# Moving the sums of a later stage from the stretches of two heads to those of two convolution groups

## The chip, the cores and the metric

The kernel runs on one core of a Trainium2 chip. The metric is device time in microseconds, the median of several executions of the whole program. One further execution was profiled; the trace and the profile page come from it. The engines are called as in the profile: PE (matrix products; PEld is its weight load), DVE, ACT, POOL, and SP, which only issues DMAs here.

## The reference

One layer of a hybrid decoder, on a sequence of 2048 rows of width 1024 with 16 learned rows in front. What is computed, cut to what matters:

```
hn   = rms_norm(h, norm1_g)
proj = einsum('bld,de->ble', hn, w_in)              # 1024 x 4096
cx, cb, cc, cg, q, k, v, rg = split(proj, 8)        # 512 columns each
conv_out = short_conv(cx, cb, cc, conv_w) * silu(cg)
qf, kf   = rotary(q) * 128**-0.5, rotary(k)
ret      = head_group_norm(retention_chunkwise(qf, kf, v), ret_norm_g)
mixed    = concat([conv_out, ret * silu(rg)])       # 1024 wide
h        = h + einsum('ble,ed->bld', mixed, w_out)
out      = rms_norm(h, final_g)[:, 16:]
```

Everything is float32. There are four retention heads of width 128, and the convolution half is worked in four groups of 128 channels.

## The kernel before

**Stages.** The sequence is worked in two rounds of 1024 rows, and then comes an output stage of eight pairs of 128-row tiles for `w_out`. A round has eight units: four heads (units 0 to 3, function `head`) and four convolution groups (units 4 to 7, function `conv_group`; unit 4 of the first round is `group_plain`). The order is (4, 0, 1, 2, 3, 5, 6, 7) in the first round and (0, ..., 7) in the second. A unit is two products of 256 columns of `w_in` with the 1024 rows, called quads. The profile has a quad's matmuls at line 215.

**Products.** Each float32 operand is split into a high part (ACT, line 102) and a low part (DVE, line 114 or 106), and three matmuls stand for one. A quad also saves one product in eight by a scheme of block sums (function `quad`, seven products of 12 matmuls): it needs sums and differences of the four blocks of each operand. On the side of the weights they are made for every quad, by POOL (function `stationary`, lines 136 to 139). On the other side they are made once for each 1024 rows: by `block_sums` (lines 167 to 182), which for each of four slices takes four blocks of 128x512 and makes four DVE operations of 128x512, and one scaling on ACT if a gain is to be applied.

**The sums of a later stage.** For the second round, and for the output stage, these sums are made ahead. The generator `prepare` (lines 184 to 192) makes one of four steps each time it is advanced: four loads of 256 KB, `block_sums`, and four stores to a DRAM buffer (line 191). In the first round it runs over the second half of the sequence (`sums_x`, with gain), in the second round over `w_out` (`sums_w`, no gain). `prepared` (lines 194 to 202) reads the buffers back at the start of the stage that uses them. For half of `sums_w` the second round's last unit has early copies into SBUF (tile `held`, line 892).

**Advancing it.** `later` is that generator. It is advanced in the loop over the units (lines 881 to 883), twice after each head but unit 0; it has four steps, so the calls after units 1 and 2 use them up and the calls after unit 3 do nothing. A head ends, as written, with the loads for the next unit and with its retention part, which runs on the engines beside the next unit's products. What is written down after a head, too, stands ahead of the next unit's instructions, and runs in that unit's stretch. Another generator, `steps` (line 867), makes the row factors of the second round in the first round's convolution groups: eight loads and eight squares on ACT (line 324) a group, at units 5 and 6.

**Order on the engines.** Every engine and SP work their instructions in a fixed order, made when the program is built: a planner simulates the program, and takes on each engine, among what it holds to be ready, what was written down first. So an instruction can run ahead of what was written before it if that isn't ready. All DMAs are issued by SP.

**Buffers.** The loads, the products of heads (`kv`, `qg`), and the tiles of the convolution (`u`, `c`) and of the row factors (`n`) share 16 buffers of one tag (`GEN`, function `gen`). Weights have 8 raw buffers (`RAW`), and three for each split part (`RING`).

Of the kernel before, what the change touches and what calls it, by code (L numbers as in the profile page):

```python
# [20 lines left out]
NG = 4  # L21
# [50 lines left out]
def hybrid_trunk(ctx: ExitStack, tc: tile.TileContext, t, out: bass.AP, chunk_decay):  # L72
# [23 lines left out]
    def brief(name="b"):  # L96
        return sb.tile([P, HB + 128], F32, name=name, tag="b", bufs=BRIEF)[:, :HB]
# [50 lines left out]
    def parts(m, i, kt, src, factor=None):  # L148
        hi, lo = operand(i, kt)
        split(hi, lo, src, factor)  # L150
        m[i].append((hi, lo))

    def moving(load, scale=None, after={}):


        m = [[] for _ in range(8)]
        blocks = []
        for j in range(2):
            for half in range(2):
                for kt in range(KH):  # L160
                    k = half * KH + kt
                    blocks.append(load(k, j))
                    parts(m, BLOCK[half][j], kt, blocks[-1], scale(k) if scale else None)
                    after.get((j, k), lambda: None)()
        return m, blocks

    def block_sums(b11, b12, b22, b21, t1, t3, f, g, eng=nc.vector):

        def less(out, a, factor, b):
            if factor is None:
                sub(nc.vector, out, a, b)
            else:
                nc.vector.scalar_tensor_tensor(out=out, in0=a, scalar=factor, in1=b, op0=ALU.mult, op1=ALU.subtract)

        if f is not None:
            nc.scalar.mul(b11, b11, f)
        less(t1, b12, f, b11)
        less(b22, b22, g, t1)  # L180
        less(b21, b21, g, b22)
        sub(eng, t3, b22, b11)
# [60 lines left out]
    def plain_part(n, load, slot):  # L243
        a = sb.tile([P, HB], F32, name="ra", tag="ra", bufs=RAW)
        load(a)
        hi, lo = operand(slot, n)
        split(hi, lo, a)
        return a, (hi, lo)

    def plain_parts(loads, slot=PLAIN_W):  # L250
        w = {n: plain_part(n, loads[n], slot)[1] for n in (0, 2, 1, 3)}
        return [w[n] for n in range(4)]
# [91 lines left out]
    def row_tile(name, pair):  # L344
        return sb.tile([P, BLK], F32, name=name, tag=f"rr{pair}", bufs=2)

    def row_factors(r, f):

        f.extend([row_tile("rr", r), row_tile("rr2", r), []])
        for j in range(2):  # L350
            ss = small.tile([P, 2, CH], F32, name="ss", tag="ss")
            for c in range(CH):
                row_squares(ss, r, j, c)
                yield
            f[2].append(spread_factors(ss, *(a[:, j * HB : (j + 1) * HB] for a in f[:2])))
        yield

    def gain_of(k):
        return gain[:, k : k + 1]

    def load_x(r):
        def load(k, j):
            a = gen("x")[:, :HB]
            nc.sync.dma_start(a, t["xT"][r, j, k])
            return a

        return load
# [25 lines left out]
    def meta_products(blocks, early=False):  # L393

        bank = ps_misc()
        four = [bank[i * 32 : i * 32 + NMETA, :P] for i in range(4)]
        with tc.high_priority(offset=HIGH) if early else nullcontext():
            for kt in range(KH):
                for i in (3, 2, 1, 0):
                    nc.tensor.matmul(  # L400
                        four[i], meta_s[:, i % 2 * KH + kt, :], blocks[i][:, kt * P : (kt + 1) * P],
                        start=kt == 0, stop=kt == KH - 1,
                    )
        scratch = sb.tile([P, HB], F32, name="mk", tag="tc", bufs=COPIES).rearrange("p (a c) -> p a c", a=CH)
        for i in range(4):
            nc.scalar.copy(out=scratch[:NMETA, i], in_=four[i])
        return scratch
# [30 lines left out]
    def w_loads(n):  # L438
        return [lambda a, i=i: nc.sync.dma_start(a, t["w_in"][n, i]) for i in range(4)]
# [375 lines left out]
    for r in range(NR):  # L815
        f = factors[r]
        rot_t = sb.tile([P, 2, BLK], F32, name="rot_t", tag="rot_t", bufs=1)
        p0 = NMETA + r * BLK

        def load_tables():  # L820
            nc.sync.dma_start(rot_t, t["rot"][:, :, p0 : p0 + BLK])

        if r == 0:
            w = [None] * 4
            loads = w_loads(2 * NG)

            def begin(half):
                for n in (half, 2 + half):
                    w[n] = plain_part(n, loads[n], FIRST_W)

            m, b = moving(
                load_x(r), gain_of, {(0, 0): lambda: begin(0), (0, KH - 1): lambda: begin(1), (0, KT - 1): normalise_meta}
            )
            first = [[p for a, p in w]]
            blocks = None, meta_products([a for a, p in w])
            first.append(plain_parts(w_loads(2 * NG + 1)))
            load_tables()
            nc.sync.dma_start(cols, t["cols"])
            t3 = [a[:, i * HB : (i + 1) * HB] for a in (row_tile("t3", 1) for _ in range(2)) for i in range(2)]
            t1 = [brief("t1") if n < BRIEF else sb.tile([P, HB], F32, name="t1", tag="tc", bufs=COPIES) for n in range(KH)]  # L840
            for kt in range(KH):
                b11, b21, b12, b22 = (b[n * KH + kt] for n in range(4))
                block_sums(b11, b12, b22, b21, t1[kt], t3[kt], gain_of(kt), gain_of(KH + kt), nc.gpsimd)
                parts(m, 2, kt, b22)
                parts(m, 6, kt, b21)
            for _ in row_factors(0, f):
                pass
            nc.sync.dma_start(causal, t["causal"])
            nc.sync.dma_start(conv_w, t["conv_w"])
            nc.sync.dma_start(ret_g, t["ret_norm_g"])  # L850

            def late_parts():
                for i, held in ((3, t1), (4, t3)):
                    for kt in range(KH):
                        parts(m, i, kt, held[kt])

            between = ()
            later = prepare(load_x(1), sums_x, gain_of)
        else:
            m, b = moving(load_x(r), gain_of)  # L860
            first = [plain_parts(w_loads(0))]
            load_tables()
            prepared(m, sums_x, (1, 3))
            between = (lambda: prepared(m, sums_x, (0, 2)),)
            blocks = None, None
            later = prepare(load_w_out, sums_w)
        steps = row_factors(r + 1, factors[r + 1]) if r < NR - 1 else iter(())
        units = UNITS[r]
        turning = None
        special = (first, between)  # L870
        for n, unit in enumerate(units):
            following = units[n + 1] if n + 1 < len(units) else None
            rest = lambda: ahead(r, following, early=n == 0)
            if r + n == 0:
                blocks, completion = group_plain(unit - NG, m, f, blocks[1], first, late_parts, rest)
                special = (), completion
            elif unit < NG:
                if turning is None:
                    turning = [row_tile(name, 1 - r) for name in ("apart", "across")]
                blocks = head(unit, r, m, rot_t, f, turning, blocks, rest, *(special if unit == 0 else ()))  # L880
                if unit > 0:
                    next(later, None)
                    next(later, None)
            else:
                if r == NR - 1 and following is None:
                    idle = sb.tile([P, 2, BLK], F32, name="held", tag="rot_t", bufs=1)
                    areas = [idle[:, 0], idle[:, 1], row_tile("held", 0), row_tile("held", 0)]
                    for i, a in enumerate(areas):
                        for j in range(2):
                            n, kt = 2 * (i // 2), i % 2 * 2 + j  # L890
                            held[n, kt] = a[:, j * HB : (j + 1) * HB]
                            nc.sync.dma_start(held[n, kt], sums_w[n, kt])
                blocks = conv_group(unit - NG, r, m, f, blocks, rest)
                for _ in range(4 - r):
                    next(steps, None)

    m, b = moving(load_w_out)
    final_g = row_tile("final_g", 1)
# [41 lines left out]
```

## Time and profile before

| | us |
|---|---|
| median of 3 runs (lowest to highest) | 887.29 (886.79 to 888.18) |
| the profiled execution's own time | 886.64 |
| its span, from the first to the last instruction | 884.9 |
| PE busy | 872.3 |
| DVE busy | 718.4 |
| POOL busy | 400.4 |

The granted clock of TensorE was 0.999 on average. The span is what the trace shows; the profiled execution's time has 1.7 us more around it. PE's matmuls are pipelined: one of line 215 has a duration of about 390 ns in the trace and the next starts 227 ns after it, so PE can show as busy while a matmul starts up to 0.16 us late.

Rows of a table by stretches are read like this: the stretch in us from the start of the span, its length, then for PE, PEld, DVE, ACT and POOL the busy time with the number of instructions in brackets, the granted clock, the share of the DMA engines, and GB/s. Rows of groups have line, engine, operation, tile written, tiles read, shapes and count, then busy time and mean ns of one, then the idle time before them and what ended it. Rows of the timeline begin with start and duration in us.

### The profile page before, as it was taken

The numbers are of one execution on the slowest core, as the hardware profiler recorded it, in microseconds if no ns is written. First come the engines' busy times: TensorE is split into PE (matmuls) and PEld (weight loads), VectorE is DVE, ScalarE is ACT, GpSimd is POOL, SyncE is SP. The second block draws the span as 40 slices with busy tenths as digits, with TensorE's granted clock in tenths as the row PEclk, the third lists the DMA queues.
The fourth block names the chain that finished last, engine by engine and source line by source line (L and its number), as shares of the span: only waits on it lengthen the run. The fifth ranks groups of instructions, "written<-read, shape, count | busy, mean of one in ns | idle before, by whom it ended". The sixth has DMA issues, their size and how long they took to land.

```text
span 884.9 us, 12802 instructions
## 1 busy us (share of the span) xinstructions
PE 872.3 (99%) x4343; PEld 717.7 (81%) x4343; DVE 718.4 (81%) x1176; ACT 441.1 (50%) x848; POOL 400.4 (45%) x291
## 2 busy tenths in 40 slices
PE   8999999999999999999999999999999999999996
PEld 5778788878888878888888888888888887788885
DVE  6888888989877866999899999877768699767763
ACT  8664426354545463836352534444334475555553
POOL 0554232323235554452223333354546445887773
PEclk9999999999999999999999999999999999999999
DMA  9721216455334343834236363325222493545531
GB/s 338 234 65 50 73 49 180 142 152 170 90 101 145 107 144 95 288 113 135 58 85 215 88 223 96 119 71 155 60 72 60 145 366 108 175 159 175 171 129 74
DMA packets 93137, 121.12 MB, mean 137 GB/s; under 512 B 24528, under 2 KB 41232, under 8 KB 93072
## 3 DMA queue, kind: packets, MB, share of 16 engines
q1 hardware_dynamic: 93072, 120.31, 43.0%
q8 instruction: 34, 0.56, 0.3%
q14 instruction: 31, 0.25, 0.1%
HBM read 90.92 MB, written 25.17 MB: 131 GB/s over the span
## 4 chain that ended last, share of the span: by engine, by line
PE 56%; DVE 6%; DMA 2%; issue 2%; ACT 1%; POOL 1%; SPq 0%; POOLq 0%; DVEq 0%; ACTq 0%
PE pj L215 50%; DVE ml L114 2%; PE pj L265 2%; DVE wl L114 1%; PE ms L682 1%; PE ms L669 1%; DVE ml L106 1%; PE ms L693 1%; PE ms L692 1%; DMA t<-sums_w 1%; DMA n<-in_x 1%; POOL yo L111 0%; DMA yo<-in_x 0%; DMA ra<-in_w_in 0%; DVE pm L709 0%
## 5 line engine op out<-in xcount | busy, mean ns | idle before, releaser
L215 PE MATMUL pj<-mh,wl 128*128 128x512 f32 x1008 | 398.7, 396 | 1.9 <-ACT tc L222 1.0
L215 PE MATMUL pj<-ml,wh 128*128 128x512 f32 x1008 | 393.2, 390 | 0.0
L215 PE MATMUL pj<-mh,wh 128*128 128x512 f32 x1008 | 392.7, 390 | 0.0
L102 ACT CAST wh<-ra 128x512 fp32r<-128x512 f32 x216 | 133.7, 620 | 260.9 <-PE pj L215 201.3
L215 PEld LDWEIGHTS pj<-mh,wl 128*128 128x128 f32 x1008 | 189.3, 188 | 44.7 <-ACT tc L222 2.8
L114 DVE TENSOR_TENSOR wl<-ra,wh 128x512 fp32r<-128x512 f32 x216 | 193.4, 898 | 39.3 <-ACT wh L102 38.9
L215 PEld LDWEIGHTS pj<-mh,wh 128*128 128x128 f32 x1008 | 189.2, 188 | 39.8
L215 PEld LDWEIGHTS pj<-ml,wh 128*128 128x128 f32 x1008 | 189.4, 188 | 37.9 <-issue 0.5
L114 POOL TENSOR_TENSOR ra<-ra 128x512 f32<-128x512 f32 x72 | 113.1, 1571 | 93.9 <-PE ms L400 40.9
L111 POOL TENSOR_TENSOR sa<-ra 128x512 f32<-128x512 f32 x36 | 55.2, 1533 | 100.0 <-DVE wl L114 46.7
L114 POOL TENSOR_TENSOR ra<-sa,ra 128x512 f32<-128x512 f32 x36 | 52.5, 1459 | 92.5 <-DVE wl L114 78.2
L222 ACT COPY tc<-pj 128x512 f32<-128x512 f32 x108 | 62.8, 581 | 0.0
L265 PE MATMUL pj<-ml,mh 128*128 128x512 f32 x128 | 50.2, 392 | 0.1
L265 PE MATMUL pj<-mh,mh 128*128 128x512 f32 x128 | 49.9, 393 | 0.0
L265 PE MATMUL pj<-mh,ml 128*128 128x512 f32 x128 | 48.8, 398 | 0.5 <-DVE ml L114 0.4
L525 POOL TENSOR_TENSOR c<-c,rr 128x512 f32<-128x512 f32 x14 | 27.8, 1984 | 26.8 <-DVE c L525 18.0
L705 POOL TENSOR_TENSOR rp<-rs,neg_half 128x4 f32<-128x4 f32 x16 | 19.4, 1215 | 43.4 <-DVE rs L111 43.4
L756 DVE TENSOR_TENSOR yo<-pj,yo 128x512 f32<-128x512 f32 x32 | 21.9, 687 | 17.9 <-PE pj L215 8.0
L102 ACT CAST wh<-sa 128x512 fp32r<-128x512 f32 x36 | 22.4, 621 | 27.5 <-PE pj L215 27.4
L761 POOL TENSOR_TENSOR z<-yo,final_g 128x512 f32<-128x512 f32 x16 | 27.0, 1687 | 16.1 <-DVE yo L756 16.1
L525 POOL TENSOR_TENSOR c<-c,tc 128x512 f32<-128x512 f32 x14 | 25.5, 1823 | 17.8 <-ACT tc L552 17.8
L758 ACT ACTIVATE rot<-yo 128x512 f32<-128x512 f32 x32 | 20.2, 630 | 26.8 <-DVE yo L756 25.8
(137 smaller groups left out, 1166.0 us busy)
## 6 DMA issues: line engine op xcount, KB each, us to landing
ra<-in_w_in SPq DMA_DIRECT2D x128, 256.0 KB, 2.7
x<-in_xT SPq DMA_DIRECT2D x48, 256.0 KB, 4.8
w<-in_w_out SPq DMA_DIRECT2D x32, 256.0 KB, 4.7
ra<-mixed SPq DMA_DIRECT2D x32, 256.0 KB, 2.9
yo<-in_x SPq DMA_DIRECT2D x32, 256.0 KB, 4.6
ra<-in_x SPq DMA_DIRECT2D x16, 256.0 KB, 3.2
mixed<-c SPq DMA_DIRECT2D x16, 256.0 KB, 2.5
mixed<-qg SPq DMA_DIRECT2D x16, 256.0 KB, 2.4
```

The costliest lines, as they stand in the source:

```text
L102: nc.scalar.copy(out=hi, in_=src)
L106: nc.vector.scalar_tensor_tensor(out=lo, in0=src, scalar=scale, in1=hi.bitcast(F32), op0=ALU.mult, op1=ALU.subtract)
L111: eng.tensor_tensor(out=out, in0=a, in1=b, op=ALU.add)
L114: eng.tensor_tensor(out=out, in0=a, in1=b, op=ALU.subtract)
L215: nc.tensor.matmul(bank, a[:, ks], b, start=first and kt == 0 and n == 0, stop=kt == KH - 1 and n == 2, skip_group_check=not first,)
L222: copied[0] = nc.scalar.copy(out=c, in_=bank)
L265: nc.tensor.matmul(banks[i], a[:, ks], b, start=half + kt + n == 0, stop=half == 1 and kt == KH - 1 and n == 2,)
L525: eng.tensor_tensor(out=out, in0=a, in1=b, op=ALU.mult)
L705: nc.gpsimd.tensor_tensor(out=rp, in0=rs, in1=neg_half.rearrange("p (c a) -> p c a", a=1), op=ALU.pow)
L756: last[0] = nc.vector.tensor_tensor(out=y, in0=pp, in1=y, op=ALU.add)
L758: nc.scalar.activation(junk, y, AF.Square, accum_out=ss[:, i, j : j + 1])
L761: nc.gpsimd.tensor_tensor(out=ys[i][j], in0=y, in1=final_g[:, j * HB : (j + 1) * HB], op=ALU.mult)
```

## The change

The two calls that advance `later` move out of the branch of the heads, to the end of the loop's body, under another condition: after unit 3 and every convolution group, but not after the first unit of the first round.

```diff
                 blocks = head(unit, r, m, rot_t, f, turning, blocks, rest, *(special if unit == 0 else ()))
-                if unit > 0:
-                    next(later, None)
-                    next(later, None)
             else:
...
                 blocks = conv_group(unit - NG, r, m, f, blocks, rest)
                 for _ in range(4 - r):
                     next(steps, None)
+            if NG - 1 <= unit and r + n > 0:
+                next(later, None)
+                next(later, None)
```

`NG` is 4. The four steps are used up by the first two units that meet the condition: units 3 and 5 in the first round, units 3 and 4 in the second. By the order described above they are then written ahead of units 5 and 6, and of units 4 and 5. In the first round the second two steps come after the `steps` of unit 5. Loads, arithmetic, stores and their number stay the same, as do the readers of the buffers.

## The prediction

> **What bounds the kernel now.** First the page's busy shares, then the idle time of PE, then the chain of waits, then one table of stretches.
>
> ```profile
> span 884.9 us, 12802 instructions
> PE 872.3 (99%) x4343; PEld 717.7 (81%) x4343; DVE 718.4 (81%) x1176; ACT 441.1 (50%) x848; POOL 400.4 (45%) x291
> ```
>
> PE is idle for 884.9 - 872.3 = 12.6 us in all. A table by stretches (length, then busy time of PE, PEld, DVE, ACT and POOL, each with its instructions in brackets) says where:
>
> ```profile
> 0.00:148.40 148.40, 144.52 (x780) 114.13 (x781) 125.04 (x215) 83.09 (x171) 50.95 (x41) 1.00 0.44 141
> 148.40:764.00 615.60, 614.02 (x3065) 509.70 (x3064) 515.17 (x857) 297.68 (x557) 266.70 (x187) 1.00 0.43 135
> 764.00:884.90 120.90, 113.73 (x502) 93.84 (x500) 78.18 (x106) 60.30 (x122) 82.79 (x65) 0.99 0.43 142
> ```
>
> In the first stretch 3.88 us are idle and in the last 7.17. Both lie outside what the change touches: the sums that it moves start at 151 us and are read by 764. Between them, in 615.6 us, PE is idle for 615.60 - 614.02 = **1.58 us**. That is all that a relief of any other engine can win as visible idle time.
>
> Busy need not mean moving at full pace, so I look at the chain of work for a long run of one kind:
>
> ```profile
> 579.26 122.45 PE pj L215 x540
> ```
>
> 122.45 us / 540 = 0.2268 us per matmul, with nothing else in between, through most of four convolution groups of the second round. A group has 2 x 84 such matmuls, 38.1 us, so these stretches stand at the pace of PE itself.
>
> Now the units one by one, cut where PE begins a unit's first product. First round: units 1, 2, 3 (heads) and 5, 6 (convolution groups); second round: units 1, 2, 3 and 4, 5. `later` is advanced after a head has been written down, so its work falls in the stretch of the unit that follows: today in units 2 and 3 of each round.
>
> ```profile
> 98.90:148.40 49.50, 49.26 (x285) 41.26 (x284) 44.74 (x90) 21.92 (x43) 14.21 (x12) 1.00 0.37 104
> 148.40:197.60 49.20, 49.20 (x285) 41.15 (x284) 43.16 (x90) 23.23 (x45) 14.87 (x12) 1.00 0.45 140
> 197.60:247.35 49.75, 49.32 (x286) 41.14 (x284) 44.98 (x92) 23.23 (x45) 14.22 (x12) 1.00 0.43 130
> 247.35:296.24 48.89, 48.53 (x277) 40.31 (x275) 36.57 (x80) 27.72 (x60) 23.60 (x21) 1.00 0.43 130
> 296.24:338.65 42.41, 42.41 (x207) 33.12 (x206) 29.45 (x43) 22.79 (x49) 24.69 (x20) 1.00 0.36 112
> 422.20:469.60 47.40, 47.32 (x249) 40.02 (x248) 40.81 (x75) 21.66 (x38) 14.59 (x10) 1.00 0.36 103
> 469.60:516.60 47.00, 47.00 (x250) 40.10 (x248) 43.83 (x84) 20.86 (x37) 16.54 (x10) 1.00 0.51 156
> 516.60:563.60 47.00, 47.00 (x249) 40.06 (x248) 43.77 (x84) 20.84 (x37) 17.14 (x11) 1.00 0.40 122
> 563.60:606.30 42.70, 42.70 (x211) 36.02 (x210) 35.38 (x66) 17.91 (x27) 19.86 (x15) 1.00 0.39 115
> 606.30:644.40 38.10, 38.10 (x169) 31.53 (x169) 26.79 (x32) 14.11 (x24) 21.47 (x17) 1.00 0.27 80
> ```
>
> The row to hold on to is the second round's: unit 1 carries no sums and takes 47.40 us, units 2 and 3 carry them and take 47.00 each. DVE is busier there, and PE isn't slower. In the first round it is 49.50 without against 49.20 and 49.75 with. So today the sums cost PE at most some tenths of a microsecond.
>
> **The change part by part.** Nothing is computed differently; two pairs of steps a round move, from the stretches of units 2 and 3 to those of 5 and 6 (first round) and of 4 and 5 (second). A pair of steps issues 8 loads, 8 stores and 8 sums on DVE, and in the first round 2 scalings on ACT as well.
>
> *What leaves the heads.* The DVE groups, the first two rows for 148 to 216 us alone, the last for the whole run:
>
> ```profile
> L175 DVE SCALAR_TENSOR_TENSOR x<-x,gain 128x512 f32<-128x512 f32 x12 | 10.9, 910 | 2.6 <-ACT x L178 2.5
> L114 DVE TENSOR_TENSOR x<-x 128x512 f32<-128x512 f32 x4 | 2.7, 681 | 0.0
> L114 DVE TENSOR_TENSOR w<-w 128x512 f32<-128x512 f32 x16 | 12.6, 821 | 0.0
> ```
>
> First round: 10.9 + 2.7 = 13.6 us, 6.8 a pair. Second round: 12.6 us, 6.3 a pair. The head stretches fall to 43.16 - 6.8 = 36.4 and 38.2 us of DVE, and to 37.5 each in the second round. On the path this wins only what PE waits for there. The table of waits from 148.4 to 764 us names what it found, and the first row is the one in a stretch with sums:
>
> ```profile
> PE ms L692 <- DVE pm L684: 0.4, 1, 0.4
> PE pj L215 <- DVE wl L114: 0.4, 1, 0.4
> PE pj L215 <- ACT tc L222: 0.4, 1, 0.4
> ```
>
> That one is at 215 us in unit 3: idle 49.75 - 49.32 = 0.43 us, behind a full DVE queue with three sums in it. The timeline of DVE there, with the POOL and SP rows beside it:
>
> ```profile
> 207.11 1.70 DVE L175 SCALAR_TENSOR_TENSOR x<-x,gain 128x512 f32<-128x512 f32 x1
> 211.23 0.75 DVE L175 SCALAR_TENSOR_TENSOR x<-x,gain 128x512 f32<-128x512 f32 x1
> 211.90 0.68 DVE L114 TENSOR_TENSOR x<-x 128x512 f32<-128x512 f32 x1
> 214.71 0.75 DVE L684 SCALAR_TENSOR_TENSOR pm<-ms,cols,causal 128x512 f32<-128x512 f32 x1
> ...
> 206.96 1.29 POOL L111 TENSOR_TENSOR sa<-ra 128x512 f32<-128x512 f32 x1 [5.51 <-DMA ra<-in_w_in]
> ...
> 203.28 3.19 SPq L191 DMA_DIRECT2D sums_x<-x  x4
> 206.57 0.40 SPq L439 DMA_DIRECT2D ra<-in_w_in  x1
> ```
>
> Without 1.70 + 0.75 + 0.68 = 3.1 us ahead of it, pm would have been early. **Term 1: -0.43 us.** What is late next is the matmul itself, at its own pace.
>
> *What comes to the convolution groups.* DVE there: unit 5, 36.57 + 6.8 = 43.4 of 48.89 us (89%); unit 6, 29.45 + 6.8 = 36.3 of 42.41 (85%); second round unit 4, 35.38 + 6.3 = 41.7 of 42.70 (**98%**); unit 5, 26.79 + 6.3 = 33.1 of 38.10 (87%). The heads carry 93% today (43.83 of 47.00) with PE not idle, so three of the four fit by that measure, and one is above anything these rows show. The sums run early in a stretch, so I look at the first 24 us of the stretches that hold them now, and then of those that get them:
>
> ```profile
> 148.40:172.40 24.00, 24.00 (x136) 20.70 (x135) 20.84 (x44) 11.20 (x25) 9.84 (x8) 1.00 0.46 160
> 516.60:540.60 24.00, 24.00 (x131) 20.59 (x130) 23.01 (x52) 7.25 (x12) 7.63 (x5) 1.00 0.49 161
> ...
> 247.35:271.35 24.00, 24.00 (x137) 20.93 (x136) 16.12 (x37) 10.12 (x24) 8.98 (x8) 1.00 0.29 89
> 296.24:320.24 24.00, 24.00 (x107) 19.57 (x105) 16.66 (x22) 10.06 (x18) 12.43 (x12) 1.00 0.30 91
> 563.60:587.60 24.00, 24.00 (x129) 20.61 (x128) 18.82 (x47) 7.87 (x13) 7.33 (x6) 1.00 0.38 110
> 606.30:630.30 24.00, 24.00 (x107) 19.87 (x107) 16.29 (x21) 9.51 (x16) 12.22 (x11) 1.00 0.32 93
> ```
>
> With the sums: 22.9, 23.5, 25.1 and 22.6 us of DVE in 24. 23.01 went without a wait of PE. Only unit 4 of the second round overflows, by 25.1 - 23.0 = 2.1 us, and the rest of its stretch (18.70 us long, 35.38 - 18.82 = 16.56 busy) has 2.1 us of room, the next unit 5.0 more. The cost lies between 0, if the overflow moves back, and 6.3 us, if PE waits out a whole pair; below 0 it could go by the 0.36 us that PE idles in unit 5 of the first round (48.89 - 48.53), but nothing in added DVE work would remove that wait; in the other three PE is busy throughout. I take 0.4, the size of the only wait that four such pairs have caused so far. **Term 2: +0.4 us.**
>
> *Other queues.* ACT gets 2 x 0.75 us in each of units 5 and 6, where it is busy 27.72 of 48.89 and 22.79 of 42.41: nothing, as long as they stay clear of 281 to 288 us, where the squares for the next round fill it and the third wait above (0.4 us) arises. SP gets 16 issues a pair, about 0.4 and 0.3 us each, 5.6 us; weight loads queue behind its stores (206.57 above, POOL idle 5.51 us) and PE did not notice; the convolution groups have as many weight loads, and I take 0. The readers of the sums: the second pair of the first round would end near 320 us, where its first reader is issued at 366.8, 46 us of cover; in the second round near 630, where the early copies are issued from 564.8 today and must now wait, but their first use is at 739:
>
> ```profile
> L201 SPq DMA_DIRECT2D t<-sums_x x8: 320/327/668, 366.8 to 377.3; - x8
> L892 SPq DMA_DIRECT2D held<-sums_w x8: 332/424/503, 564.8 to 604.1; - x8
> L102 ACT CAST mh<-held x8: 602/616/617, 739.3 to 744.0; 128x512 fp32r<-128x512 f32 x8
> ```
>
> 109 us of cover: 0. If the planner holds SP for those copies, weight loads would be late too; that belongs to the first rival.
>
> *A rule against the change.* The sum at 207.11 took 1.70 us and ended 0.56 us after the POOL add of 206.96 (end 208.25); its like at 211.23 took 0.75. The Trainium skill, SBUF — State Buffer, on the shared port pair, states that a VectorE instruction with two SBUF inputs and a GpSimd instruction that reads SBUF exclude each other for the whole instruction. By that rule the sums would be dearer in the new place; this trace agrees, 1.70 against 0.75. From the rows alone: POOL is busy 12.43 and 12.22 of 24 us in the places of the second pairs, 9.84 and 7.63 in those of today, so about one more collision of 0.95 us a round, on a DVE with 0.5 to 1.4 us left of its 24. It is no term of the sum, but part of the first rival's price.
>
> Sum: the profiled execution took 886.64 us (span 884.9 and 1.7 around it); -0.43 + 0.4 leaves 886.6. The median of the three runs is 0.65 us above that execution, so the forecast is **887.3**.
>
> **The rivals.**
> - *DVE becomes the bound in unit 4 of the second round, slower.* Sums are written down ahead of that group's weight splits and product reads, and come first on DVE when both are ready. For it: 98%, and 25.1 us in 24. Against it: units 2 and 3 had the same order at 93 to 96% and PE lost nothing. It decides once what PE waits for is more than the 2.1 us of room late. Price 2.1, up to 6.3, and 0.5 to 1 for collisions: 889.4 to 893.6, at the likeliest 889.9. Chance 0.15.
> - *The second pair of the first round meets the squares.* If its loads wait for buffers, its scalings and stores share ACT and SP with the squares around 281 to 288 or 318 to 325 us, where PE has waited for ACT already. Two to four scalings of 0.75 us: +1.5 to 3.0, 889 to 890. Chance 0.06.
> - *Relief in the heads shows.* All of the 1.58 us gone: 885.7, which is 0.18% and still no difference. For more, matmuls would have to be held up without an idle gap showing; 47.40 without sums against 47.00 with them speaks against it. Chance of over 0.2%: 0.05.
> - *The change doesn't do what it says*, since the planner may issue ahead of the written order (the copies at 564.8 belong to unit 7, which starts at 682.5). Then 887.3 again, 0.06.
>
> **How the numbers follow.** A measurement of this kernel can tell about 0.2%, 1.8 us, from no change: 885.5 to 889.1. The forecast has 0.68; with the fourth rival 0.74 for no difference. Of the first two rivals, 0.21 together, all count as slower; faster has 0.05. The range goes from 885.8, nearly all idle time won, to 890.2, past the likeliest price of the first rival.
>
> **What would show it.** Right: the stores to `sums_x` between about 250 and 325 us and to `sums_w` between about 570 and 635; PE at 0.227 us per matmul and 42.7 and 38.1 us for units 4 and 5 of the second round; the wait for pm at 215 us gone; DVE near 37 us in the heads. Wrong: a wait of PE for wl, a product read or tc in 564 to 610 us or near 285 us; units 2 and 3 shorter than 47.0, which would mean hidden waits; copies of `sums_w` not landed by 739.

## The result, and the profile after

The changed kernel takes 893.11 us (893.00 to 893.57 in four runs) against 887.26 (886.79 to 888.18): 1.0068 times the time before, interval 1.0055 to 1.0080. That is 5.85 us slower, outside the predicted range. The profiled execution took 893.22 us, its span is 891.4. Here and below, ratios and intervals are the record's own estimates over the undisturbed executions, so a ratio isn't always the quotient of the two medians; one execution of experiment 5 (5028 us) and one of experiment 12 (970.5 us at a granted clock of 0.85) count in the medians only.

The page of the changed kernel, and the table by stretches, cut at the same places of the program as before:

```profile
span 891.4 us, 12807 instructions
PE 873.1 (98%) x4343; PEld 717.3 (80%) x4343; DVE 720.3 (81%) x1176; ACT 441.9 (50%) x848; POOL 398.0 (45%) x291
```

```profile
0.00:149.00 149.00, 144.25 (x780) 114.02 (x781) 125.08 (x215) 83.22 (x171) 51.34 (x41) 1.00 0.41 131
149.00:770.60 621.60, 615.10 (x3065) 509.46 (x3064) 517.47 (x857) 298.34 (x557) 264.09 (x187) 1.00 0.43 136
770.60:891.40 120.80, 113.75 (x502) 93.84 (x500) 77.74 (x106) 60.34 (x122) 82.61 (x65) 0.99 0.44 142
```

PE has the same work, but in the middle stretch it now idles for 621.60 - 615.10 = 6.50 us where it idled for 1.58. Of the 6.5 us by which the span grew, 4.92 are there; 0.87 more are in the first stretch (4.75 for 3.88), which the change doesn't touch; PE's busy time grew by 0.8. The table of waits of PE, 149 to 770 us of the changed kernel, names the waits:

```profile
PE pj L215 <- DVE tc L111: 2.3, 2, 1.5
PE pj L215 <- DVE wl L114: 2.1, 2, 1.2
PE pj L215 <- ACT tc L222: 1.0, 1, 1.0
PE pj L215 <- ACT tc L552: 0.7, 1, 0.7
```

All six, 6.1 us, stand in two places: 287 to 305 us (the end of unit 5 of the first round and the beginning of unit 6) and 601 to 611 us (the end of unit 4 of the second). The rows by unit: unit 5 of the first round; units 2, 3, 4 and 5 of the second.

```profile
247.04:298.43 51.39, 48.83 (x277) 40.24 (x276) 44.42 (x92) 30.32 (x64) 22.69 (x20) 1.00 0.74 246
...
472.37:519.42 47.05, 47.05 (x250) 40.03 (x248) 39.07 (x76) 21.14 (x37) 14.25 (x10) 1.00 0.26 68
519.42:566.48 47.06, 47.06 (x249) 40.03 (x248) 38.98 (x76) 21.14 (x37) 14.25 (x10) 1.00 0.34 99
566.48:613.23 46.75, 43.88 (x211) 35.78 (x210) 44.92 (x81) 17.77 (x27) 20.48 (x15) 1.00 0.70 227
613.23:651.40 38.17, 38.17 (x169) 31.47 (x168) 27.55 (x33) 14.01 (x24) 22.80 (x18) 1.00 0.38 111
```

The heads lost 4.8 us of DVE work each (6.3 had been counted) and won nothing: 47.05 and 47.06 us where they took 47.00. Unit 4 grew from 42.70 to 46.75 us, and its DVE work from 35.38 to 44.92 us, by far more than the 6.3 us of one pair. Unit 5, for which the prediction had counted the second pair, has hardly more than before (27.55 for 26.79). The stores of the sums say the same, first those of `sums_x`, then those of `sums_w`:

```profile
L191 SPq DMA_DIRECT2D sums_x<-x x16: 319/327/1125, 251.6 to 298.5; - x16
L191 SPq DMA_DIRECT2D sums_w<-w x16: 319/320/1646, 570.5 to 609.0; - x16
```

Both pairs ended inside one unit, 566.5 to 613.2 us in the second round. The timeline of DVE there, start and duration:

```profile
598.28 0.68 DVE L114 TENSOR_TENSOR w<-w 128x512 f32<-128x512 f32 x1
598.88 0.68 DVE L111 TENSOR_TENSOR tc<-pj,tc 128x512 f32<-128x512 f32 x1
599.48 1.19 DVE L114 TENSOR_TENSOR w<-w 128x512 f32<-128x512 f32 x1
600.60 1.77 DVE L114 TENSOR_TENSOR wl<-ra,wh 128x512 fp32r<-128x512 f32 x1
602.29 0.68 DVE L525 TENSOR_TENSOR tc<-tc,rr 128x512 f32<-128x512 f32 x1
602.89 3.00 DVE L114 TENSOR_TENSOR w<-w 128x512 f32<-128x512 f32 x3
605.81 0.68 DVE L114 TENSOR_TENSOR wl<-ra,wh 128x512 fp32r<-128x512 f32 x1
```

There is no gap in it, and three sums (602.89, 3.00 us) stand between two splits of weights (wl) that PE waits for. Some of these operations take 1.2 to 1.8 us where their likes take 0.68. So far the trace. It leaves open which of three things costs: the place of the second pair, the amount, or the transfers that come with it.

### The profile page after: what moved, and what is told of

Same layout as the page of the kernel before. It is cut to its first block, busy times and chain, and to the rows that moved or that the text cites. A ratio compares the mean times of both kernels' runs of the same rounds, so it can differ in the third digit from the quotient of the medians.

```text
span 891.4 us, 12807 instructions
## 1 busy us (share of the span) xinstructions
PE 873.1 (98%) x4343; PEld 717.3 (80%) x4343; DVE 720.3 (81%) x1176; ACT 441.9 (50%) x848; POOL 398.0 (45%) x291
## 4 chain that ended last, share of the span: by engine, by line
PE 75%; DVE 9%; DMA 4%; issue 2%; POOL 1%; ACT 1%; SPq 0%; POOLq 0%; DVEq 0%; ACTq 0%
PE pj L215 65%; PE pj L265 2%; DMA w<-in_w_out 2%; PE ms L682 1%; DVE ml L114 1%; PE ms L669 1%; PE ms L693 1%; PE ms L692 1%; DVE wl L114 1%; DVE w L114 1%; DMA t<-sums_w 1%; PE ms L654 1%; PE ms L659 1%; DMA n<-in_x 1%; PE ms L400 1%
## 5 line engine op out<-in xcount | busy, mean ns | idle before, releaser
L114 DVE TENSOR_TENSOR wl<-ra,wh 128x512 fp32r<-128x512 f32 x216 | 190.2, 882 | 41.8 <-ACT wh L102 41.4
L102 ACT CAST wh<-sa 128x512 fp32r<-128x512 f32 x36 | 22.3, 620 | 31.4 <-PE pj L215 31.4
L525 POOL TENSOR_TENSOR c<-c,tc 128x512 f32<-128x512 f32 x14 | 26.5, 1890 | 21.3 <-ACT tc L552 21.3
L525 POOL TENSOR_TENSOR c<-c,rr 128x512 f32<-128x512 f32 x14 | 27.1, 1934 | 18.3 <-DVE c L525 9.3
```

Of the source, the lines that this page charges most:

```text
L102: nc.scalar.copy(out=hi, in_=src)
L114: eng.tensor_tensor(out=out, in0=a, in1=b, op=ALU.subtract)
L525: eng.tensor_tensor(out=out, in0=a, in1=b, op=ALU.mult)
```

## The experiments

Each experiment's time is compared with the kernel before on the same chip, whose median was 887.24 us for experiments 1 to 4, 887.30 for 5 to 8, 887.17 for 9 and 10 and 887.94 for 11 and 12.

**1. Both pairs behind heads, one beside a convolution group.**

```diff
-            if NG - 1 <= unit and r + n > 0:
+            if unit in (NG - 2, NG - 1):
```

> The first pair of steps is written behind unit 2 and the second behind unit 3, so the second runs beside a convolution group (unit 5, then unit 4), and none is written behind a convolution group. Theory A (the sums of the pair written behind the convolution group start early, run at the tail of that group's second product on a DVE that is full there, and hold up weight splits and product reads): that pair is gone, so 886.5 to 888. Theory B (two pairs in one unit are too much DVE work, wherever they stand): also 886.5 to 888. Theory C (sums beside a convolution group cost by themselves, some 3 us a pair): 889 to 891.

890.82 us (888.99 to 891.66), ratio 1.0040, interval 1.0027 to 1.0053. Theories A and B are not enough: no sum stands at a tail and no unit has two pairs, and still 3.6 us are lost. Nor is C right, for in the first round the pair beside unit 5 costs nothing that its trace shows; the only new wait in this trace is in unit 4 of the second round, at 599 us (the second number is the count):

```profile
PE pj L215 <- ACT tc L222: 2.2, 1, 2.2
```

The traced execution took 889.50 us, so its trace shows the cheaper end: the three dearer executions (890.8 to 891.7) have a mean granted clock of 0.995 or 0.996, the traced one 0.998.

**2. The second pair one unit later.**

```diff
-            if NG - 1 <= unit and r + n > 0:
+            if unit == NG - 1 or unit == (NG + 2 if r == 0 else NG + 1):
```

> The first pair stays behind unit 3; the second is written behind the second convolution group of the round (unit 6, then unit 5), one unit later than in the changed kernel. Theory A (tail of the group): the second pair again stands at the tail of a convolution group, 891 to 894, with waits of PE for wl or product reads near 320 to 340 and 640 to 652 us. Theory B (two pairs in one unit): each unit has one pair, 886.5 to 888.5.

892.35 us (890.76 to 894.27), ratio 1.0062, interval 1.0044 to 1.0080. Its trace has waits for wl of 1.65 us at 343.7 and 1.04 us at 641.9, right behind the end of unit 6 of the first round (338.1, its sums from 329.6 to 342.9) and before that of unit 5 of the second (648.9), and one for tc of 0.87 us at 600. B falls; A holds as a part, beside the wait of the first experiment.

**3. The second pair's sums behind the group's last product read.**

```diff
+                with tc.issue_after(taken[0].ins) if unit >= NG else nullcontext():
+                    next(later, None)
+                    next(later, None)
```

(`taken[0]` is the last instruction of line 559, on DVE.)

> As the changed kernel, but on DVE each sum of the second pair stands behind the last product read of the convolution group behind which it is written; loads and scalings on ACT are free to start as before. Theory A: the waits for wl and product reads at the tails (1.55 + 0.71 us in the first round, 2.86 us in the second) go, the wait for tc near 287 us may stay: 887 to 888.5. Theory C: still 891 to 894.

Ten runs, 887.50 to 892.75, median 891.88; ratio 1.0037, interval 1.0022 to 1.0052. Holding the sums back doesn't cure it. The profiled execution was the fastest of the ten (887.50). It has waits of 1.44 us for tc at 286 and 0.46 us for wl at 308, and no wait in unit 4 of the second round, although the whole first pair stands beside that unit; it doesn't show the loss of the others. What differs between them is on record only as the mean granted clock: 0.997 to 0.999 in the runs under 890, 0.995 or 0.996 in the six above 891.

**4. The second pair without its sums.**

```diff
-            block_sums(b11, b12, b22, b21, b12, b11, f, g)
+            if kt < 2:
+                block_sums(b11, b12, b22, b21, b12, b11, f, g)
```

> The changed kernel with the sums (4 DVE operations a step, in the first round one scaling on ACT too) of the second pair left out; its loads and stores stay. Theories A and B: DVE is what is overfull, so 886.5 to 888. Theory D (SP and the DMAs: weight loads queue behind the second pair's loads and stores): still 891 to 894.

889.54 us (888.22 to 890.56), ratio 1.0029, interval 1.0019 to 1.0040: in between. The waits of the first round are gone from its trace. In the second, PE waits 2.15 us at 597 us, although only the first pair's sums are left. So one pair beside unit 4 can be enough, as in experiment 1. And this trace shows a second cost. Its table of stretches, from that wait on (length, PE's busy time and count, ..., granted clock third from the end):

```profile
597.40:600.10 2.70, 0.55 (x3) 0.47 (x3) 1.50 (x2) 2.19 (x5) 1.79 (x2) 0.99 1.04 391
600.10:603.50 3.40, 3.40 (x9) 2.62 (x9) 1.69 (x3) 2.88 (x3) 0.00 (x0) 0.50 1.03 349
603.50:606.90 3.40, 3.40 (x16) 2.79 (x16) 2.55 (x4) 0.62 (x1) 0.64 (x1) 1.00 0.79 258
```

For 3.4 us after the wait the granted clock is 0.50; 9 matmuls fall in the stretch, and 16 in the next one of the same length: about 1.6 us more.

**5 and 6. One round changed, the other as before.**

```diff
+            if (NG - 1 <= unit and n > 0) if r == 0 else unit in (1, 2):    # first round only
+            if unit in (1, 2) if r == 0 else NG - 1 <= unit:                # second round only
```

> The first round as in the changed kernel (pairs behind units 3 and 5), the second as before (behind units 1 and 2). If the two rounds' costs add, the waits of the changed trace at 287, 294 and 304 us (1.01 + 1.55 + 0.71 us) less those that go (0.43 at 215, 0.36 at 287) make +2.5 us: 889 to 890.5. If the loss needs both rounds, or belongs to the second alone: 886.5 to 888.

> The second round as in the changed kernel (pairs behind units 3 and 4), the first as before. Adding: +2.9 us of waits at 601 to 610, in some executions half clock after them: 889.5 to 891.5. If the loss belongs to the first round: 886.5 to 888.

First round only: 889.00 us, ratio 1.0023, interval 1.0013 to 1.0033. Second round only: 891.58 us, ratio 1.0051, interval 1.0034 to 1.0068. The two add up to 1.0074; the whole change has 1.0068. As far as the intervals tell, the losses are separate, and the second round's is the larger. The trace of experiment 6 has waits of 0.97, 1.11 and 0.73 us at 599 to 608, less than the 4.3 us that are lost.

**7. First round only, with the second pair held back on DVE and on ACT.**

```diff
+                with (
+                    tc.issue_after(taken[0].ins) if held_back else nullcontext(),
+                    tc.issue_after(copied[0].ins) if held_back else nullcontext(),
+                ):
```

> As the one before the last, but the second pair's sums on DVE stand behind the last product read of unit 5, and its scalings on ACT behind the last bank copy of unit 5, so that they run in unit 6 and not at the tail of unit 5. Theory A (the tail is the wrong place): the waits at 287 to 304 us fall back to the 0.4 us of before, 886.5 to 888. If 13.6 us of sums beside units 5 and 6 are too much wherever they stand: 889 to 890.5.

Ten runs from 886.35 to 891.22, median 889.02; ratio 1.0016, interval 1.0004 to 1.0029. Four are at 887.4 or below. In the traced execution the waits at 287 to 304 us are down to 0.13 and 0.33, and a new one for wl, of 2.10 us, stands at 308, again with the granted clock at 0.50 for 3.4 us behind it. So the place at the tail wasn't all, here either.

**8. Experiment 1 without the sums beside unit 4.**

```diff
-            block_sums(b11, b12, b22, b21, b12, b11, f, g)
+            if scale or kt < 2:
+                block_sums(b11, b12, b22, b21, b12, b11, f, g)
```

> Pairs behind units 2 and 3 in both rounds, as in the first experiment (890.8), but in the second round the pair that stands beside unit 4 has its 8 sums left out; loads and stores stay. Theory E (one pair of sums, 6.3 us, beside unit 4 makes DVE late for the silu and the split behind it, and PE waits about 2.2 us near 599): the wait goes, 886.5 to 888. Theory D (its loads and stores do it): 889 to 891.5.

887.23 us, ratio 0.9995, interval 0.9986 to 1.0005, and no wait of PE in unit 4. The loads and stores cost nothing; what the sums do on DVE does. D falls.

**9. Experiment 1 without POOL's work beside it.**

```diff
-        quad(stationary(blocks), m, take)
+        quad(stationary(blocks, r == 0 or g != 1), m, take)
...
-        quad(stationary(load_raw(w_loads(n))), m, take)
+        quad(stationary(load_raw(w_loads(n)), r == 0 or g != 0), m, take)
...
+                if r == 0 or g != 0:
+                    mul(nc.gpsimd, cs[j], cs[j], rr[j])
+                    mul(nc.gpsimd, cs[j], cs[j], c)
```

(With False, `stationary` splits unsummed blocks in place of the sums that POOL makes.)

> Pairs behind units 2 and 3, as in the first experiment (890.8), but in the second round the block sums that POOL makes of the weights of unit 4's second and unit 5's first product, and the two products of 128x512 on POOL in each half of unit 4's second product, are left out; DVE's own work is the same. Theory F (DVE has room, but about four of its operations there take 1.78 us for 0.74 because POOL is at work beside them, and that is what makes PE wait): the wait near 599 us goes, 886.5 to 888. Theory E (the amount of DVE work alone): a wait of 1 us or more stays, 888.5 to 891.5.

887.10 us, ratio 0.9996, interval 0.9987 to 1.0006: the loss is gone with all of DVE's sums in place. DVE's rows at the beginning of unit 4's second product, in experiment 1:

```profile
590.28 3.95 DVE L462 SCALAR_TENSOR_TENSOR c<-u,conv_w,c 128x512 f32<-128x512 f32 x4
594.14 1.78 DVE L114 TENSOR_TENSOR wl<-sa,wh 128x512 fp32r<-128x512 f32 x1
595.85 0.68 DVE L111 TENSOR_TENSOR tc<-pj,tc 128x512 f32<-128x512 f32 x1
596.45 1.40 DVE L114 TENSOR_TENSOR wl<-ra,wh 128x512 fp32r<-128x512 f32 x1
597.77 1.78 DVE L525 TENSOR_TENSOR tc<-tc,rr 128x512 f32<-128x512 f32 x1
```

POOL at the same time:

```profile
589.77 1.75 POOL L114 TENSOR_TENSOR ra<-ra 128x512 f32<-128x512 f32 x1
593.64 1.73 POOL L525 TENSOR_TENSOR c<-c,rr 128x512 f32<-128x512 f32 x1 [1.41 <-DVE c L462]
596.00 1.30 POOL L111 TENSOR_TENSOR sa<-ra 128x512 f32<-128x512 f32 x1 [0.63 <-DVE wl L114]
597.38 1.62 POOL L114 TENSOR_TENSOR ra<-ra 128x512 f32<-128x512 f32 x1
```

And DVE's same instructions in experiment 9 (its line 533 is line 525 there, 470 is 462):

```profile
591.00 2.76 DVE L470 SCALAR_TENSOR_TENSOR c<-u,conv_w,c 128x512 f32<-128x512 f32 x4
593.68 0.68 DVE L114 TENSOR_TENSOR wl<-ra,wh 128x512 fp32r<-128x512 f32 x1
595.03 0.69 DVE L111 TENSOR_TENSOR tc<-pj,tc 128x512 f32<-128x512 f32 x1 [0.67 <-PE pj L223]
595.66 0.69 DVE L114 TENSOR_TENSOR wl<-ra,wh 128x512 fp32r<-128x512 f32 x1
596.27 0.68 DVE L533 TENSOR_TENSOR tc<-tc,rr 128x512 f32<-128x512 f32 x1
```

Four operations that start while POOL is at work are 3.95 - 2.76 + 1.10 + 0.71 + 1.10 = 4.1 us longer. Each ends shortly after POOL's does: 594.14 + 1.78 = 595.92, POOL's 593.64 + 1.73 = 595.37. The last of them, `tc`, is what the silu on ACT waits for; the bank copy that PE needs stands behind the silu on ACT. In experiment 9 DVE even has a gap there. One reservation: leaving out POOL's sums also takes away the splits' wait for them. In experiment 1 DVE has no gap between 585.6 and 599.5 us, so no such wait held it up there.

**10. Half a pair beside unit 4.**

```diff
+            if 1 <= unit <= 3:
+                for _ in range(2 if unit == 1 else 1):
+                    next(later, None)
```

> Two steps behind unit 1, one behind unit 2, one behind unit 3, in both rounds: half a pair (4 sums, 3.2 us) beside unit 4 in place of 6.3 us. Theory E with a threshold of about 2 us of room: the wait near 599 is under 1 us and the half clock after it doesn't come, 887 to 888.5. If any sum beside unit 4 sets off the same chain of late operations: 889 to 891.5.

886.93 us, ratio 1.0000, interval 0.9990 to 1.0009, and no wait in unit 4. DVE there, and one row of POOL:

```profile
586.61 1.62 POOL L114 TENSOR_TENSOR ra<-ra 128x512 f32<-128x512 f32 x1 [0.68 <-POOL ra L114]
...
589.75 2.73 DVE L462 SCALAR_TENSOR_TENSOR c<-u,conv_w,c 128x512 f32<-128x512 f32 x4
592.40 0.68 DVE L114 TENSOR_TENSOR wl<-sa,wh 128x512 fp32r<-128x512 f32 x1
593.12 0.69 DVE L111 TENSOR_TENSOR tc<-pj,tc 128x512 f32<-128x512 f32 x1
593.76 1.03 DVE L114 TENSOR_TENSOR wl<-ra,wh 128x512 fp32r<-128x512 f32 x1
594.71 1.77 DVE L525 TENSOR_TENSOR tc<-tc,rr 128x512 f32<-128x512 f32 x1
```

Two operations out of these are lengthened and not four. The kernel before, without any sums here, has the same five durations, the last of them

```profile
594.58 1.77 DVE L525 TENSOR_TENSOR tc<-tc,rr 128x512 f32<-128x512 f32 x1
```

and PE doesn't wait. So lengthened operations were there before the change, too. Nor is DVE later with a whole pair: the first `c` begins 2.26 us after the product's first matmul in experiment 1 (588.02), 2.34 us here (587.41). What differs is POOL: its sum `ra` is over before `c` begins here (586.61), and runs beside `c` in experiment 1 (589.77). By the times the limit lies between 3.2 and 6.3 us of sums early in that unit; whether it is their amount, or the other order on POOL that came with the whole pair in experiments 1 to 4, no run separates.

The traces of experiments 1 to 4 settle what makes PE wait. All four have a whole pair of sums beside unit 4, and work these five rows in the same order from `c` to `tc` (L525; L526 in experiment 4). The durations in us, and PE's wait behind them:

| | c (4) | wl | tc | wl | tc | start of c to end of the last tc | PE's wait |
|---|---|---|---|---|---|---|---|
| before | 2.73 | 0.68 | 0.69 | 1.03 | 1.77 | 6.73 | none |
| experiment 3 | 3.95 | 0.68 | 0.68 | 1.18 | 0.68 | 6.85 | none |
| experiment 2 | 3.94 | 0.68 | 0.68 | 1.18 | 1.77 | 7.94 | 0.87 |
| experiment 4 | 3.93 | 1.78 | 0.68 | 1.40 | 1.77 | 9.25 | 2.15 |
| experiment 1 | 3.95 | 1.78 | 0.68 | 1.40 | 1.78 | 9.27 | 2.16 |

From experiment 2 to experiment 4 the stretch grows by 1.31 us and the wait by 1.28. Experiment 3 has the same starts as experiment 1 as far as the first `wl`; from there, with the row of POOL that runs beside it last:

```profile
594.14 0.68 DVE L114 TENSOR_TENSOR wl<-sa,wh 128x512 fp32r<-128x512 f32 x1
594.75 0.68 DVE L111 TENSOR_TENSOR tc<-pj,tc 128x512 f32<-128x512 f32 x1
595.35 1.18 DVE L114 TENSOR_TENSOR wl<-ra,wh 128x512 fp32r<-128x512 f32 x1
596.45 0.68 DVE L525 TENSOR_TENSOR tc<-tc,rr 128x512 f32<-128x512 f32 x1
...
593.64 2.33 POOL L525 TENSOR_TENSOR c<-c,rr 128x512 f32<-128x512 f32 x1 [1.53 <-DVE c L462]
```

Here POOL's operation is the longer one (2.33 us for 1.73) and DVE's keeps its 0.68. So the same sums cost 2.16 us of waiting or none, by which of the two engines is held up.

**11. One step behind each of four units.**

```diff
+            if 2 <= unit <= 6 and unit != (4 if r == 0 else 2):
+                next(later, None)
```

> One step behind each of units 2, 3, 5, 6 in the first round and behind each of units 3, 4, 5, 6 in the second: four sums of DVE (3.4 or 3.2 us) a stretch, three of the four steps of a round beside convolution groups. If what costs is the amount in one place (half a pair beside unit 4 cost nothing): 886.5 to 888. If sums that follow a convolution group cost in any amount: 889 to 892.

890.86 us, ratio 1.0033, interval 1.0021 to 1.0045. So at the tail of a convolution group half a pair is too much already: the trace has waits of 0.51, 0.44 and 0.42 us for wl at 603, 642 and 681 us, in the three units of the second round behind which a step is written, and 1.22 and 0.61 at 287 and 294. The step beside the beginning of unit 4 (568.8 to 572 us) has none behind it.

**12. Experiment 5 without POOL's work beside the end of unit 5.**

```diff
+        quad(stationary(blocks, r == 1 or g != 2), m, take)
...
+        quad(stationary(load_raw(w_loads(n)), r == 1 or g != 1), m, take)
...
+                if r == 1 or g != 1:
```

> The first round as in the changed kernel, the second as before (889.0 so far), and POOL's block sums of the weights of unit 5's second and unit 6's first product, and its two products of 128x512 in each half of unit 5's second product, left out. If the loss of the first round, too, comes from DVE operations lengthened by POOL: 886.5 to 887.8. If there the eight sums themselves stand ahead of what PE waits for, whatever POOL does: 888 to 889.5.

885.91 us against 887.94, ratio 0.9978, interval 0.9969 to 0.9987. The loss of the first round goes as well, and some more with it, which wasn't followed up; so what is left out here wins something besides, and the trace says more than the time. DVE's order at the tail is the same in both; in experiment 5 it begins with

```profile
287.44 1.77 DVE L288 TENSOR_TENSOR rot<-ident,rc 128x512 f32<-128x512 f32 x1
...
294.33 0.67 DVE L111 TENSOR_TENSOR tc<-pj,tc 128x512 f32<-128x512 f32 x1
```

and in experiment 12 with

```profile
286.69 0.68 DVE L296 TENSOR_TENSOR rot<-ident,rc 128x512 f32<-128x512 f32 x1
...
292.48 0.69 DVE L111 TENSOR_TENSOR tc<-pj,tc 128x512 f32<-128x512 f32 x1
```

The kernel before has the first of these lengthened, too, but no sums between it and `tc`, and PE didn't wait for that `tc`:

```profile
288.05 1.79 DVE L288 TENSOR_TENSOR rot<-ident,rc 128x512 f32<-128x512 f32 x1
```

The queue has no gap from the one row to the other in experiment 5. The 1.1 us by which the first operation is longer reach the product read `tc` undiminished, five sums further on, and PE waits 1.51 us for it there, 0.30 in experiment 12.

## Why the prediction was wrong

- *PE bounds the kernel, and a relief of the heads wins next to nothing*: right. Units 2 and 3 of the second round took 47.00 us with the sums and 47.05 and 47.06 without.
- *Term 1, -0.43 us, the wait for pm at 215 us*: right. It is gone in the changed kernel, and there, 0.58 us, in experiment 1, where a pair is beside unit 3 again.
- *The stretches of units 5 and 6, 4 and 5*: the step that failed first. The prediction put the second pair into the unit behind the group it follows, as it had been behind a head (the sums of the second pair began at 519.9 us, 3.3 us into unit 3). Behind a convolution group they began at 598.3 us, 15 us before the unit's end at 613.2. The loads of a pair need 8 of the 16 shared buffers. A head's keys, values, queries and gates hold 8 until its retention part is done, and a convolution group holds fewer, so loads came at 590.5 us, right at the beginning of the group's second product. That the buffers are what let them start was read from code and trace, not tried; SP's row before them, two transposes, also ended just there (584.85 + 5.60 = 590.45).
- *Term 2, +0.4 us*: the step that cost the forecast. It measured 6.1 us of waits, 1.55, 1.01 and 0.71 in the first round and 0.96, 1.16 and 0.74 in the second, where the kernel before had 0.36, for tc at 287. It was sized by the one wait that the sums had caused beside heads, and the collisions with POOL were left out of the sum, as "part of the first rival's price", at one more of 0.95 us a round. Experiment 1 has 4.1 us of them in one place. It takes both the sums and the collisions: without the sums (8) or with half of them (10) nothing is lost beside unit 4, although POOL's work is there, and without POOL beside them (9, and 12 for the first round) the same sums cost nothing.
- *The first rival* had the engine and the unit: a pair beside unit 4 costs 3.6 us (experiment 1), and half of one nothing. Its ground was wrong. The 25.1 us of DVE work in the first 24 us of unit 4 came out as 22.26 us in 23.98 (566.48 to 590.46) with no wait of PE, in part since operations that had been lengthened there no longer were (`u`, 1.76 us at 571.38 before, 0.68 at 576.97 after): busy times that hold such lengthening don't add up. The 98% for the whole unit came out as 38.57 us in 43.08, 90%, in experiment 3, with no wait. PE waits later, by the collisions in the second product, of which the rival had 0.5 to 1 us. That its price of 2.1 to 6.3 us holds the 4.3 us that the second round lost (experiment 6) is therefore in good part luck.
- *The second rival*, the meeting with the squares at 281 to 288 us: the two scalings came, at 286.5 and 288.1 us, and the wait for tc there is 1.01 us for 0.36. That they made it longer isn't shown: experiment 5, with the same two scalings, has 0.48 us, and experiment 6, whose first round is as before, 0.83. The larger loss of that place was on DVE.
- *The readers of the sums have cover*: right. PE has no wait for `sums_x` or `sums_w` in the changed kernel's middle stretch, and the last early copy of `sums_w`, issued at 614.5 us, is far ahead of the first use at 746.3. That SP's issues cost nothing was right as well, as far as experiment 8 shows it, beside unit 4.
- *The rule of the Trainium skill on the shared port pair (SBUF — State Buffer, Who interferes with whom)*: the trace of experiment 1 agrees with it, with four lengthened operations that ended within 0.6 us after POOL's (the first `c` at 592.07 after 591.52, then 595.92 after 595.37, 597.85 after 597.30, 599.55 after 599.00). Taken as a term, it would have pointed the right way.

What stays open: how much of the second round's 4.3 us (experiment 6) is the second pair at the tail and how much the first pair's chain, since 9 was made with one pair only; whether the sums' amount or POOL's other order brings the collisions about; and what makes the untraced executions of experiments 3 and 7 differ, beyond the granted clock.

## What to carry to other kernels

That an engine is at 93% of a stretch without a visible cost doesn't say what more work will cost: look at what stands behind it in its own queue, and whether another engine lengthens its operations there. Where work moves, ask what it waits for in the new place (its buffers, the queue that issues its loads), for its place in the code alone didn't say when it started. And busy times that hold such lengthening don't add up: a stretch reckoned at 25.1 us in 24 held 22.3, and the cost arose behind it. Reckon with the operations that will be lengthened, and with what waits for them.

## What the runs showed of the hardware

A wait of PE of about 2.1 us can be followed by half clock, which costs about 1.6 us more: in experiments 4 and 7 the granted clock fell to 0.50 for 3.41 us, 0.5 to 0.7 us after the end of waits of 2.15 and 2.10 us. In experiment 1 a wait of 2.16 us was followed by no such thing in the traced execution, nor were the shorter waits, up to 1.65 us (experiment 2). The Trainium skill, TensorE: Matmul & The Clock Gate, in the section on HAM oscillation, gives gaps of more than about 3.4 us of idle PE as what brings the half clock; here 2.1 us were enough in two traces out of three, and the measurement decides. The granted clock of the untraced executions of experiment 3, 0.995 or 0.996 in all six above 891 us, fits with that (3.41 us at half clock are 0.002 of the mean), but wasn't traced.
